# A head norm's sums issued behind the next product, row maxima spaced one by one, and their transposes some products later

## The chip, the cores and the metric

The kernel runs on one core of one Trainium2 chip. The metric is the device time of one execution in microseconds; of several runs the median is given, with the lowest and the highest.

## The reference

One inference step of a small hybrid model, on a prompt of 1024 tokens and a sample of 32 new tokens that has 1024 cached ones. Layer 0 mixes tokens with a state-space scan, layer 1 with multi-head latent attention; a gated per-layer embedding follows each. The change concerns the prompt's attention in layer 1 alone. Cut to what matters (16 heads, 64 plain and 32 rotated columns of a query or key, chunks of 64 tokens):

```python
q = (rmsnorm(q_a, q_a_norm) @ q_b_w).reshape(b, T, MLA_HEADS, MLA_QK)
q_nope = rmsnorm(q[..., :MLA_NOPE], qn_norm)
q_rope = apply_rope(rmsnorm(q[..., MLA_NOPE:], qr_norm), cos[:, None], sin[:, None])
kv = (lat_all @ kv_b_w).reshape(b, Tk, MLA_HEADS, MLA_NOPE + MLA_V)
k_nope = rmsnorm(kv[..., :MLA_NOPE], kn_norm)
...
s = (jnp.einsum('bqhd,bkhd->bhqk', qn, k_nope)
     + jnp.einsum('bqhd,bkd->bhqk', qr, k_rope)).astype(F32) * scale
mask = k_chunk[None, :] <= (qp // CHUNK)[:, None]
p = jax.nn.softmax(jnp.where(mask, s, -jnp.inf), axis=-1).astype(v.dtype)
return jnp.einsum('bhqk,bkhd->bqhd', p, v)
```

So each head's query and key are normed per token over the head's columns (the head norm), and each query's scores need the maximum of its row before the exponential.

## The kernel before, in words

**Numbers.** Nearly all products are of fp32 operands split into a high part that TensorE takes in one pass and a low rest (names with h and l, types fp32r): high by high, high by low and low by high are summed. A matmul on plain fp32, such as the norm's sum, shows as two records in the trace.

**Stages.** Layer 0, its output and its embedding fill the span up to 1078 us; then comes the attention's input projection, then `phase_sample` (the sample's attention), then `phase_prompt`, the prompt's, and after it the output projection and the last embedding.

**The order of work.** The kernel's text emits instructions; a scheduler then fixes the order on each engine. It plans along a simulated time and takes, of what is ready, what was emitted first. So the order of emission sets priorities, not the order itself. Buffers are given out by tag: tiles of one tag share `bufs` places, and a tile waits until a place is free. In the prompt's attention PSUM has four tags of two banks each: "mm" (products of preparation, the sums of head norms, values), "st" (scores), "s1" (row-max products and the transposes of maxima) and "o" (outputs).

**Preparation.** `Prompt.prep(p)` makes queries and keys of head pair p: two weights, two halves of 512 tokens each, so four products. For each, `gemm` (L245) fills a bank, `head_sq` (L900, L901) has ScalarE copy it to `hx` and square it to `hsq`, and `head_norm` (L910 to L913) sums the squares over each head by a matmul with a block-diagonal matrix into another bank of "mm", takes the reciprocal root on ScalarE (a logarithm and an exponential, L182 and L183) and multiplies on VectorE. `Prompt.rope_block(g)` does the same for the rotated columns of four heads (two products), then swaps halves by eight DMAs on SyncE and rotates. Both are generators that yield after each product. The first pair's preparation runs inside `phase_sample`, with products in the tag "st" there.

**Operands.** Two sets of buffers `qk` alternate between pairs. `fill(p)` puts the prepared halves into them: ScalarE writes the high parts (L1263), a DMA on GpSimd's queue the rotated rows (L1264), VectorE or GpSimd the low parts (L1268).

**Row maxima.** `row_max(i, par)` treats one head: for each of 8 blocks of 128 queries, one or two products of high parts (L1307), each followed by a maximum on VectorE (L1309): twelve in all, four blocks with one, four with two. It yields after each block, eight times. At its end a small reduction (L1311), a transpose on TensorE (L1313), a copy with the sign turned on ScalarE (L1315) and a DMA on GpSimd's queue (L1316) put the row of maxima into the low query operand `ql`, as a row of its own, so that the score product subtracts it.

**A head.** `head` walks twelve pieces: three score products (L1327), the exponential on ScalarE (L1333), the high part `ph` on ScalarE or VectorE (L1345, L1347), the rest `pl` on GpSimd or VectorE (L1348), three products with the values (L1350 to L1352; one fp32 product at L1341 for two of the eight key blocks). It yields after each piece.

**Interleaving.** For each pair p, `spread` merges three streams by position: the 24 pieces of pair p, the row maxima of pair p+1 (16 steps), and the preparation of pair p+2 (4 steps, 6 with a rope block). Step k of n stands at (k + 0.5)/n, less a lead of 0.05 for the last two. What a stream has left then runs in `run`, at the end. After odd pairs `values` (L1279) makes the values of the next four heads.

Of the kernel before, what the change touches and what calls it, by code (L numbers as in the profile page):

```python
# [10 lines left out]
F32 = mybir.dt.float32  # L11
# [6 lines left out]
P = 128  # L18
# [136 lines left out]
class Pools:  # L155


    def __init__(self, rest, **tags):
        self.rest, self.tags = rest, tags
# [32 lines left out]
def load_weight(c, src, nk, m, scale=None, eng_h=None, wp=None, wr=None):  # L192
    nc = c.nc
    wp = wp or c.wp
    raw = (wr or wp).tile([P, nk, m], F32, tag="wraw", name="wraw")
    nc.sync.dma_start(raw, src)
    if scale is not None:
        nc.gpsimd.tensor_tensor(raw, raw, bc_last(scale, m), op=ALU.mult)
    wh = wp.tile([P, nk, m], F32R, tag="wh", name="wh", bufs=c.whb)
    wl = wp.tile([P, nk, m], F32R, tag="wl", name="wl", bufs=c.whb)  # L200
    if eng_h:
        eng_h.tensor_copy(wh, raw)
    else:
        nc.scalar.activation(wh, raw, AF.Copy)  # L204
    nc.gpsimd.tensor_tensor(wl, raw, wh.bitcast(F32), op=ALU.subtract)  # L205
    return wh, wl
# [55 lines left out]
def pvc(c, name, i=0, n=1, rows=P):  # L262
    o, _ = PV[name]
    return c.pv[:rows, o + i : o + i + n]
# [631 lines left out]
def head_sq(c, ps, x, pool=None):  # L896

    n = x.shape[-1]
    sq = (pool or c.pre).tile([P, 352 if pool else 512], F32, tag="hsq", name="hsq", bufs=2)[:, :n]
    c.nc.scalar.activation(x, ps, AF.Copy)  # L900
    c.nc.scalar.activation(sq, ps, AF.Square)  # L901
    return sq


def head_norm(c, x, sq, w, bd):

    nc = c.nc
    n = x.shape[-1]
    pn = c.ps.tile([P, 512], F32, tag="mm", name="hn", bufs=2)
    nc.tensor.matmul(pn[:, :n], bd[0], sq, start=True, stop=True)  # L910
    r = c.pre.tile([P, 512], F32, tag="hr_", name="hr_", bufs=2)
    rsqrt(nc, c, r[:, :n], pn[:, :n], 1.0 / bd[1], c.eps)
    nc.vector.scalar_tensor_tensor(x, x, w, r[:, :n], op0=ALU.mult, op1=ALU.mult)  # L913
# [248 lines left out]
class Prompt:  # L1162


    def __init__(self, c, st):
        self.c, self.st, self.x = c, st, {}
        self.tag = "st"

    def rope_block(self, g):
        c, nc, I = self.c, self.c.nc, self.c.I  # L1170
        w = load_weight(c, I["qrW"][g], 3, P)
        rope = c.pre.tile([P, 2, 1024], F32, tag="rope", name="rope")
        sw, fq = rope[:, 0], rope[:, 1]
        for a in range(2):
            cols = slice(512 * a, 512 * a + 512)
            ps = c.ps.tile([P, 512], F32, tag=self.tag, name="psr", bufs=2)
            gemm(c, ps, w, self.st.qan, cols)
            head_norm(c, fq[:, cols], head_sq(c, ps, fq[:, cols]), pvc(c, "qr"), (c.bd32, 32))
            yield
        for h in range(4):  # L1180
            lo, hi = slice(32 * h, 32 * h + 16), slice(32 * h + 16, 32 * h + 32)
# [12 lines left out]
        nc.scalar.activation(h, fq, AF.Copy)  # L1194
        nc.vector.tensor_tensor(l, fq, sw, op=ALU.subtract)
        self.rope = rope.bitcast(F32R)

    def prep(self, p):

        c, I = self.c, self.c.I  # L1200
        self.x[p] = out = []
        for wsrc, nk, acts, wn in ((I["qnW"][p], 3, self.st.qan, "qn"), (I["kW"][p], 2, self.st.latp, "kn")):
            w = load_weight(c, wsrc, nk, P)
            for a in range(2):
                ps = c.ps.tile([P, 512], F32, tag=self.tag, name="psqk", bufs=2)
                gemm(c, ps, w, acts, slice(512 * a, 512 * a + 512))
                x = c.pre.tile([P, 512], F32, tag="hx", name="hx", bufs=6)
                head_norm(c, x, head_sq(c, ps, x), pvc(c, wn), (c.bd64, 64))
                out.append(x)
                yield  # L1210


def run(*gens):
    for g in gens:
        for _ in g:
            pass


LEAD = 0.05


def spread(*streams):

    order = sorted(((k + 0.5) / n - lead, i) for i, (_, n, lead) in enumerate(streams) for k in range(n))
    for _, i in order:
        next(streams[i][0], None)
    run(*(g for g, _, _ in streams))


def phase_prompt(c, st, pr, before):  # L1230
    nc, tc, I, O = c.nc, c.tc, c.I, c.O
    es = ExitStack()
    ap_ = es.enter_context(tc.tile_pool(name="att", bufs=1, reuse_waits="tile"))
# [4 lines left out]
    bufs = []  # L1238
# [55 lines left out]
            out.append((vh, vl))  # L1294
        return out

    def row_max(i, par):
        qk = bufs[i]
        qh, ql, kh, kl = (qk[n][par] for n in ("qh", "ql", "kh", "kl"))
        mrow = gap_rows(par, i).start + 10  # L1300
        mx = ap_.tile([P, 16], F32, tag="mx", name="mx", bufs=2)
        for b in range(8):
            n = max(256, 128 * (b + 1))
            ng, w = (1, n) if n <= 512 else (2, n // 2)
            for a in range(ng):
                ps = c.ps.tile([P, 512], F32, tag="s1", name="s1", bufs=2)
                nc.tensor.matmul(ps[:, :w], qh[:, 128 * b : 128 * b + 128], kh[:, a * w : a * w + w], start=True, stop=True)  # L1307
                col = b if b < 4 else 2 * b + a
                nc.vector.tensor_reduce(mx[:, col : col + 1], ps[:, : (w if b else 128)], axis=AX.X, op=ALU.max)  # L1309
            yield  # L1310
        nc.vector.tensor_reduce(mx[:, 4:8], mx[:, 8:16].rearrange("p (a b) -> p a b", b=2), axis=AX.X, op=ALU.max)  # L1311
        pm = c.ps.tile([P, 512], F32, tag="s1", name="pm", bufs=2)
        nc.tensor.transpose(pm[:8, :128], mx[:, 0:8], c.ident)  # L1313
        mr = ap_.tile([8, 128], F32R, tag="mr", name="mr", bufs=2)
        nc.scalar.activation(mr, pm[:8, :128], AF.Copy, scale=-1.0)  # L1315
        nc.gpsimd.dma_start(ql[mrow : mrow + 1, :], mr)  # L1316

    def head(vt, i, par, opair):
        qk = bufs[i]
# [42 lines left out]
    def pair(p, vt, opair):  # L1362
        for par in range(2):
            yield from head(vt, p % 2, par, opair)

    operands(0)
    fill(0)
    run(row_max(0, 0))
    operands(1)
    vt = values(0)  # L1370
    run(row_max(0, 1))
    run(pr.prep(1))
    for p in range(8):
        g, i = p // 2, p % 2
        opair = ap_.tile([P, 1024], F32, tag="op", name="op")
        sg = aq.tile([P, 1024], F32, tag="sg", name="sg")
        nc.sync.dma_start(sg, c.sg_d[p][:, :1024])
        streams = [(pair(p, vt, opair), 24, 0.0)]
        if p < 7:
            fill(p + 1)  # L1380
            streams.append((itertools.chain(row_max(1 - i, 0), row_max(1 - i, 1)), 16, LEAD))
        if p < 6:
            streams.append((itertools.chain(pr.prep(p + 2), pr.rope_block(g + 1) if i == 0 else ()), 6 if i == 0 else 4, LEAD))
        spread(*streams)
        if i == 1 and p < 7:
# [8 lines left out]
def build(tc, nc, I, O, dbg=None, ngroups=8, upto=9):  # L1394
# [4 lines left out]
    with ctx:  # L1399
# [175 lines left out]
```

## Time and profile before

| what | us |
|---|---|
| median of 3 runs | 1998.89 |
| lowest, highest | 1995.81, 2002.09 |
| the profiled execution, its own time | 1996.68 |
| its span | 1994.9 |
| TensorE busy (matmuls) | 1921.6 |
| VectorE, ScalarE, GpSimd busy | 1254.2, 1051.0, 955.6 |

The profile is of one execution. PE is TensorE's matmuls, PEld its weight loads, DVE is VectorE, ACT ScalarE, POOL GpSimd, SP SyncE. L1307 is line 1307 of the kernel before. A group's row gives the engine, the operation, output and inputs by their names, shapes and count, then busy time, mean ns of one, the idle time in front of it and what ended most of that. A row of waits gives who waited for whom, the total in us, the times, the longest. A row of the order in time gives start and duration in us. Matmuls are pipelined, so that a matmul's record still runs when the next one has started.

### The profile page before, as it was taken

To read this page: it belongs to the slowest core of one execution; us is meant where nothing else is said; L and a number is where in the kernel's file an instruction comes from. 1 tells how busy PE (TensorE), PEld (TensorE's weight loads), DVE (VectorE), ACT (ScalarE), POOL (GpSimd) and SP (SyncE) were. 2 spreads that over 40 slices of the span, in tenths; PEclk is the share of its full clock that TensorE was granted. 3 is DMA by queue.
4 is the path that set the end of the run, shared out by engine and by line. 5 is a ranking of instruction groups with operands and counts; after the bars stand their busy time and mean duration, and the time that the engine had idled before them with its cause. 6 is when DMAs were issued, how large, how long until landed. Compare 5 with 4: busy or idle time off the path is not lost. (4 is left out here: it accounts for less than half of the span.)

```text
span 1994.9 us, 32715 instructions
## 1 busy us (share of the span) xinstructions
PE 1921.6 (96%) x12811; PEld 1766.3 (89%) x12811; DVE 1254.2 (63%) x1613; ACT 1051.0 (53%) x1958; POOL 955.6 (48%) x811
## 2 busy tenths in 40 slices
PE   8999999999999999999998999998999999899999
PEld 6988899999999998989998999677778777779999
DVE  7888675746657575452377443364777887976544
ACT  5436555455545557342334341777687877754331
POOL 5642524343443545555777452124445454545772
PEclk9999999999999999999999999999999999999999
DMA  4134333424233347553233221434331311316442
GB/s 141 54 86 99 87 87 104 91 78 98 74 95 88 77 119 254 161 181 122 94 125 113 84 73 69 160 107 129 78 79 43 80 40 38 121 45 199 123 130 71
DMA packets 110730, 204.26 MB, mean 102 GB/s; under 512 B 18224, under 2 KB 60720, under 8 KB 110448
## 3 DMA queue, kind: packets, MB, share of 16 engines
q1 hardware_dynamic: 105472, 193.17, 33.0%
q0 software_dynamic: 2800, 6.91, 1.8%
q8 instruction: 100, 1.64, 0.3%
q10 hardware_dynamic: 2304, 2.10, 0.3%
q14 instruction: 54, 0.44, 0.1%
HBM read 156.81 MB, written 38.83 MB: 98 GB/s over the span
## 5 line engine op out<-in xcount | busy, mean ns | idle before, releaser
L205 POOL TENSOR_TENSOR wl<-wraw,wh 128x1024 fp32r<-128x1024 f32 (+3 forms) x183 | 373.4, 2042 | 424.0 <-ACT wh L204 386.2
L245 PE MATMUL mm<-hh,wl 128*128 128x384 f32 (+1 forms) x1136 | 372.7, 328 | 0.0
L245 PE MATMUL mm<-hh,wh 128*128 128x384 f32 (+1 forms) x1136 | 372.0, 328 | 0.0
L245 PE MATMUL mm<-hl,wh 128*128 128x384 f32 (+1 forms) x1136 | 370.8, 326 | 0.0
L245 PE MATMUL pso<-yhl,wh 128*128 128x264 f32 x1536 | 282.2, 285 | 4.7 <-DVE yhl L259 2.9
L204 ACT ACTIVATE wh<-wraw 128x1024 fp32r<-128x1024 f32 (+3 forms) x181 | 157.2, 869 | 245.8 <-PE pso L245 111.6
L245 PEld LDWEIGHTS pso<-yhl,wh 128*128 128x128 f32 x1536 | 238.5, 188 | 6.2 <-DVE yhl L259 4.0
L245 PE MATMUL pso<-yhl,wl 128*128 128x264 f32 x768 | 218.6, 285 | 3.9 <-POOL wl L205 3.9
L245 PEld LDWEIGHTS mm<-hh,wh 128*128 128x128 f32 x1136 | 214.6, 189 | 3.2 <-issue 2.8
L245 PEld LDWEIGHTS mm<-hl,wh 128*128 128x128 f32 x1136 | 214.8, 189 | 1.3 <-issue 0.5
L245 PEld LDWEIGHTS mm<-hh,wl 128*128 128x128 f32 x1136 | 214.6, 189 | 0.7 <-issue 0.2
L496 DVE SCALAR_TENSOR_TENSOR cx<-raw,pv,cx 128x1060 f32<-128x1060 f32 x96 | 142.6, 1490 | 42.6 <-ACT cx L494 42.0
L245 PE MATMUL psi<-yhl,wh 128*128 128x264 f32 x832 | 154.7, 287 | 4.1 <-ACT yhl L258 3.7
L559 ACT ACTIVATE ex<-ex,tokT 128x128 f32<-128x128 f32 (+1 forms) x288 | 87.0, 380 | 132.9 <-DMA ex<-acs_d 123.8
L245 PEld LDWEIGHTS pso<-yhl,wl 128*128 128x128 f32 x768 | 144.5, 188 | 4.6 <-POOL wl L205 4.6
L245 PE MATMUL pg<-hH,wl 128*128 128x264 f32 x512 | 145.9, 285 | 1.3 <-POOL wl L205 1.3
L245 PE MATMUL pg<-hH,wh 128*128 128x264 f32 x512 | 145.9, 285 | 0.0
L245 PE MATMUL pg<-hL,wh 128*128 128x264 f32 x512 | 145.6, 285 | 0.0
L1327 PE MATMUL st<-qk 128*128 128x512 f32 (+2 forms) x576 | 139.6, 358 | 1.5 <-DMA qk<-mr 0.9
L245 PEld LDWEIGHTS psi<-yhl,wh 128*128 128x128 f32 x832 | 130.7, 190 | 5.1 <-ACT yhl L258 3.9
L1348 POOL TENSOR_TENSOR pl<-pf,ph 128x512 fp32r<-128x512 f32 x64 | 81.8, 1278 | 104.7 <-DVE ph L1347 93.8
L572 POOL TENSOR_TENSOR hm<-hT,cd_all 128x256 f32<-128x256 f32 x64 | 53.1, 830 | 162.3 <-DVE hT L574 96.1
(539 smaller groups left out, 4666.5 us busy)
## 6 DMA issues: line engine op xcount, KB each, us to landing
wraw<-in_inW SPq DMA_DIRECT2D x48, 512.0 KB, 3.5
ex<-acs_d SPq DMA_DIRECT2D x32, 512.0 KB, 5.5
wraw<-in_outW SPq DMA_DIRECT2D x32, 512.0 KB, 3.7
yraw<-y_d SPq DMA_DIRECT2D x32, 264.0 KB, 4.6
u<-u_d SPq DMA_DIRECT2D x32, 264.0 KB, 2.8
eb<-ea_d SPq DMA_DIRECT2D x64, 128.0 KB, 4.0
y_d<-y SPq DMA_DIRECT2D x16, 512.0 KB, 2.8
wraw<-in_gateW SPq DMA_DIRECT2D x16, 512.0 KB, 3.6
```

The costliest lines, as they stand in the source:

```text
L204: nc.scalar.activation(wh, raw, AF.Copy)
L205: nc.gpsimd.tensor_tensor(wl, raw, wh.bitcast(F32), op=ALU.subtract)
L245: c.nc.tensor.matmul(ps, ww[:, k, :m], aa, start=first and k == 0 and i == 0, stop=last and k == n - 1 and i == 2)
L496: nc.vector.scalar_tensor_tensor(xh, raw[:, k : k + T1], pvc(c, "cw", 4 * b + k), xh, op0=ALU.mult, op1=ALU.add)
L559: nc.scalar.activation(e_, e_, AF.Relu, scale=-1.0, bias=tok(32)[:, i, h : h + 1])
L572: nc.gpsimd.tensor_tensor(hm.rearrange("p (h q) -> p h q", q=64), hT.rearrange("p (h q) -> p h q", q=64), bc_last(cd_all[:, hs, ch], 64), ...
L1327: nc.tensor.matmul(ps[:, :n], a_[:, ks], b_[:, q], start=t == 0, stop=t == 2)
L1348: (nc.gpsimd if idx in L_POOL else nc.vector).tensor_tensor(pl[:, :n], pf[:, :n], ph[:, :n].bitcast(F32), op=ALU.subtract)
```

## The change

The head norm of a product is kept back: `norm_later` first issues the norm that is waiting, and then keeps the new one; `norm_now` issues what is left at the end of `prep` and of the two products of `rope_block`. As its arguments are worked out first, the copy and the square of a product still come right behind it; the matmul that sums the squares, the reciprocal root and the multiplication come behind the next product and its square.

`row_max` yields after each product with its maximum, twelve times a head. The transpose, copy and DMA move into `max_row`. `row_maxima` runs both heads of a pair and calls `max_row` for the first after three products of the second, and for the second after two more empty steps.

`spread` gives each stream a stretch of its own: the pieces 0 to 1, the row maxima 26 steps from -0.03 to 0.9, the preparation from -0.05 to 0.95. At the start the first twelve row maxima are issued before the operands and values, and the rest, with both transposes, behind them.

```diff
             gemm(c, ps, w, self.st.qan, cols)
-            head_norm(c, fq[:, cols], head_sq(c, ps, fq[:, cols]), pvc(c, "qr"), (c.bd32, 32))
+            self.norm_later(fq[:, cols], head_sq(c, ps, fq[:, cols]), pvc(c, "qr"), (c.bd32, 32))
             yield
+        self.norm_now()
...
-                head_norm(c, x, head_sq(c, ps, x), pvc(c, wn), (c.bd64, 64))
+                self.norm_later(x, head_sq(c, ps, x), pvc(c, wn), (c.bd64, 64))
                 out.append(x)
                 yield
+        self.norm_now()
+
+    def norm_later(self, *a):
+
+        self.norm_now()
+        self.norms.append(a)
+
+    def norm_now(self):
+        if self.norms:
+            head_norm(self.c, *self.norms.pop())
...
 def spread(*streams):
 
-    order = sorted(((k + 0.5) / n - lead, i) for i, (_, n, lead) in enumerate(streams) for k in range(n))
+    order = sorted((a + (b - a) * (k + 0.5) / n, i) for i, (_, n, a, b) in enumerate(streams) for k in range(n))
...
                 nc.vector.tensor_reduce(mx[:, col : col + 1], ps[:, : (w if b else 128)], axis=AX.X, op=ALU.max)
-            yield
+                yield
         nc.vector.tensor_reduce(mx[:, 4:8], mx[:, 8:16].rearrange("p (a b) -> p a b", b=2), axis=AX.X, op=ALU.max)
+
+    def max_row(i, par, mx):
+
+        mrow = gap_rows(par, i).start + 10
         pm = c.ps.tile([P, 512], F32, tag="s1", name="pm", bufs=2)
         nc.tensor.transpose(pm[:8, :128], mx[:, 0:8], c.ident)
         mr = ap_.tile([8, 128], F32R, tag="mr", name="mr", bufs=2)
         nc.scalar.activation(mr, pm[:8, :128], AF.Copy, scale=-1.0)
-        nc.gpsimd.dma_start(ql[mrow : mrow + 1, :], mr)
+        nc.gpsimd.dma_start(bufs[i]["ql"][par][mrow : mrow + 1, :], mr)
+
+    def row_maxima(i):
+
+        mx = [ap_.tile([P, 16], F32, tag="mx", name="mx", bufs=2) for _ in range(2)]
+        yield from row_max(i, 0, mx[0])
+        for k, _ in enumerate(row_max(i, 1, mx[1])):
+            if k == 2:
+                max_row(i, 0, mx[0])
+            yield
+        yield
+        yield
+        max_row(i, 1, mx[1])
...
     operands(0)
     fill(0)
-    run(row_max(0, 0))
+    ahead = row_maxima(0)
+    for _ in range(12):
+        next(ahead)
     operands(1)
     vt = values(0)
-    run(row_max(0, 1))
+    run(ahead)
     run(pr.prep(1))
...
-        streams = [(pair(p, vt, opair), 24, 0.0)]
+        streams = [(pair(p, vt, opair), 24, 0.0, 1.0)]
         if p < 7:
             fill(p + 1)
-            streams.append((itertools.chain(row_max(1 - i, 0), row_max(1 - i, 1)), 16, LEAD))
+            streams.append((row_maxima(1 - i), 26, -0.03, 0.9))
         if p < 6:
-            streams.append((itertools.chain(pr.prep(p + 2), pr.rope_block(g + 1) if i == 0 else ()), 6 if i == 0 else 4, LEAD))
+            streams.append((itertools.chain(pr.prep(p + 2), pr.rope_block(g + 1) if i == 0 else ()), 6 if i == 0 else 4, -0.05, 0.95))
```

More of the change, by code (lines that the diff above doesn't have):

```diff
@@ L1167, in __init__ @@
         self.tag = "st"
+        self.norms = []
     def rope_block(self, g):
@@ L1216, in run @@
             pass
-LEAD = 0.05
 def spread(*streams):
-    order = sorted(((k + 0.5) / n - lead, i) for i, (_, n, lead) in enumerate(streams) for k in range(n))
+    order = sorted((a + (b - a) * (k + 0.5) / n, i) for i, (_, n, a, b) in enumerate(streams) for k in range(n))
     for _, i in order:
         next(streams[i][0], None)
-    run(*(g for g, _, _ in streams))
+    run(*(x[0] for x in streams))
 def phase_prompt(c, st, pr, before):
@@ L1295, in values, with row_max @@
         return out
[L1297 to L1301, printed above, removed]
+    def row_max(i, par, mx):
+        qh, kh = (bufs[i][n][par] for n in ("qh", "kh"))
         for b in range(8):
```

## The prediction, made before the changed kernel was run

> **What bounds the kernel.** I read the page first: the span and the busy shares.
>
> ```profile
> span 1994.9 us, 32715 instructions
> PE 1921.6 (96%) x12811; PEld 1766.3 (89%) x12811; DVE 1254.2 (63%) x1613; ACT 1051.0 (53%) x1958; POOL 955.6 (48%) x811
> ```
>
> TensorE is busy for 96% of the span, and the change adds and removes no product. So it can only gain what TensorE waits where the change works, and lose by new waits. I then cut the span by where row-max and score products appear: the sample's attention runs up to 1394 us, a start without full pairs up to 1436, the eight pairs of heads up to 1800. The view by stretches shows these, pair 6, and a short stretch inside it.
>
> ```profile
> core 0: us, PE busy (x) PEld busy (x) DVE busy (x) ACT busy (x) POOL busy (x), PEclk, DMA share, GB/s
> 1250.00:1394.00 144.00, 132.89 (x693) 103.98 (x691) 71.71 (x135) 110.97 (x270) 39.96 (x61) 0.99 0.46 133
> 1436.00:1800.00 364.00, 347.29 (x1700) 274.92 (x1699) 290.61 (x487) 266.07 (x533) 182.69 (x189) 0.99 0.23 61
> 1724.00:1766.00 42.00, 36.32 (x173) 28.01 (x172) 39.30 (x61) 26.07 (x53) 24.77 (x23) 0.92 0.38 122
> 1737.00:1750.00 13.00, 9.51 (x32) 6.37 (x33) 12.42 (x16) 4.55 (x10) 9.49 (x6) 0.74 0.26 84
> ```
>
> The pairs take 364 us with TensorE busy in 347.29: 16.7 us idle is the order of everything that can be won there. VectorE is busy for 290.61, or 80%. In pair 6 it is 39.30 of 42, so there VectorE sets the pace. The view of waits from 1394 to 1805 tells who ended TensorE's idle time; first the matmuls' own, then the weight loads', which see a wait earlier because a matmul's tail hides the start of it.
>
> ```profile
> PE s L1307 <- DVE mx L1309: 5.4, 8, 1.6
> PE o L1351 <- POOL pl L1348: 3.0, 5, 2.1
> PE o L1350 <- DVE ph L1347: 2.5, 2, 1.8
> PE o L1351 <- DVE pl L1348: 2.5, 3, 1.5
> PE hn L910 <- ACT hsq L901: 2.2, 3, 1.0
> ...
> PEld s L1307 <- DVE mx L1309: 10.3, 18, 2.0
> PEld hn L910 <- ACT hsq L901: 3.5, 4, 1.4
> ```
>
> The change aims at two rows: row-max products that wait for VectorE's maximum (5.4 to 10.3 us) and the norm's sum that waits for ScalarE's square (2.2 to 3.5 us). The others, 8.0 us, belong to the softmax pieces, which it doesn't touch. The order on each engine is not that of the text: a scheduler fills it in from simulated times, with the order of emission as priority. The change moves emission, so it moves all of this plan.
>
> **Part 1, the norm behind the next product.** In the prompt both use the tag "mm", with two banks. In the trace a norm's sum and the next product run back to back, after the square of the product before:
>
> ```profile
> 1565.98 0.59 ACT L901 ACTIVATE hsq<-psqk 128x512 f32<-128x512 f32 x1
> 1568.53 1.02 PE L910 MATMUL hn<-hsq,bd 128*128 128x512 f32 x2
> 1568.99 0.79 PE L245 MATMUL psqk<-qanH,wh 128*128 128x512 f32 x1
> ...
> 1585.04 0.59 ACT L901 ACTIVATE hsq<-psqk 128x512 f32<-128x512 f32 x1
> 1585.69 1.13 PE L910 MATMUL hn<-hsq,bd 128*128 128x512 f32 x2 [0.95 <-ACT hsq L901]
> ```
>
> The square ends at 1566.57, the sum starts at 1568.53 and the next product at 1568.99. I read it so: product N holds one bank until its square has read it, sum N takes the other, and product N+1 needs the first. After the change the order of allocation is product N+1, sum N, product N+2, so in the steady run product N+2 still waits for square N+1: the wait of 2.2 to 3.5 us passes from the sum to a product. Gain between 0 and 3.5 us; I take 0. Only where a pair has few other products ready (as at 1585.69) would it be more. In the sample's attention the prompt's first six products use the tag "st", and there the sum really leaves their path:
>
> ```profile
> PE hn L910 <- ACT hsq L901: 3.1, 6, 1.2
> PEld hn L910 <- ACT hsq L901: 4.9, 6, 1.4
> ```
>
> Of the 30 sums in that stage 24 are the sample's own, which already come one product later, and 6 are the prompt's: a fifth of 3.1 us is 0.6. Gain between 0 and 4.9, I take 0.5. The six instructions of a norm (two matmul records, logarithm, exponential, product) stay what they are. What moves farthest is the last norm of a stream: it now comes only when the pair's other streams have been emitted, and behind it the rope's eight swaps on SyncE, its VectorE products, and the next operands' DMAs on GpSimd. Its price is in the rival on lateness.
>
> **Part 2, maxima one at a time.** Of a head's twelve products, eight came two to a step. Now each of 24 has its own step, over a stretch from -0.03 to 0.9 of the pair with two empty steps behind: the last at -0.03 + 0.93 x 23.5/26 = 0.81 of the pair instead of 15.5/16 - 0.05 = 0.92.
>
> ```profile
> L1309 DVE TENSOR_REDUCE mx<-s 128x1 f32<-128x128 f32 (+2 forms) x192 | 102.4, 550 | 26.7 <-PE s L1307 25.8
> ```
>
> A maximum takes 0.55 us and there are two banks, so two products at once leave the third waiting up to 1.1 us for VectorE, more when a cast stands ahead. At one per step this shrinks by about half, not to nothing, because VectorE stays 80% busy. Gain between 0 and 10.3; I take half of the upper row, 5.2. What is late next is the cast ph on VectorE (2.5 us above), which the same reductions delay.
>
> **Part 3, the transposes later.** Sixteen transposes, ScalarE copies and DMAs on GpSimd stay. For the first head they come at step 15 of 26 (0.49) instead of step 9 of 16 (0.48), but behind three more products; for the second, at the end of emission as before. The wait that this may spare is on GpSimd:
>
> ```profile
> L1316 POOL DMA_DIRECT2D qk<-mr x16 | 9.3, 582 | 9.1 <-ACT mr L1315 7.2 <-ACT pf L1333 1.7
> ```
>
> GpSimd sits 7.2 us in front of this DMA, and behind it in its queue stand the pl subtractions for which TensorE waits 3.0 us. Gain between 0 and 3.0, I take 0.5.
>
> **Part 4, pair 6.** There the two reductions of a step stand ahead of a cast, and TensorE runs dry:
>
> ```profile
> 1736.31 0.68 DVE L1348 TENSOR_TENSOR pl<-pf,ph 128x512 fp32r<-128x512 f32 x1
> 1738.62 1.27 DVE L1309 TENSOR_REDUCE mx<-s 128x1 f32<-128x512 f32 x2
> 1739.82 1.38 DVE L1347 CAST ph<-pf 128x512 fp32r<-128x512 f32 x1
> 1741.31 2.66 DVE L1348 TENSOR_TENSOR pl<-pf,ph 128x512 fp32r<-128x512 f32 x1
> ...
> 1741.26 0.49 PE L1350 MATMUL o<-ph,vh 128*128 128x512 f32 x1 [1.81 <-DVE ph L1347]
> 1744.02 0.80 PE L1351 MATMUL o<-pl,vh 128*128 128x512 f32 x1 [1.46 <-DVE pl L1348]
> ...
> 1740.88 2.54 POOL L205 TENSOR_TENSOR wl<-wraw,wh 128x1024 fp32r<-128x1024 f32 x1
> ```
>
> One reduction out of the way is 1.27/2 = 0.6 us: I take that, of 3.3 us (1.81 + 1.46) at most. The same pl took 0.68 us and, while a GpSimd subtraction of 2.54 us ran, 2.66. The Trainium skill (SBUF — State Buffer, "Who interferes with whom") says that a VectorE instruction with two SBUF inputs contends with a GpSimd one that reads SBUF, and that the one issued second is blocked. The trace agrees: pl was issued 0.43 us after the subtraction and ended 0.55 us after it. By that rule spacing the maxima spares nothing of the second wait, and Part 4 would stay at 0.6 at best.
>
> **The sum.** 0 + 0.5 + 5.2 + 0.5 + 0.6 = 6.8 us gained, and 0.5 us given back for last norms that come late (bounds 0 and 12, below): 6.3 net. The profiled execution took 1996.68 us, its span and 1.8 around it, and so would take 1990.4. The median of the three runs, 1998.89, is 2.2 above it, so I predict 1992.6 us. About 0.3%, 6.0 us, is what a measurement of this kernel can tell from no change.
>
> **Rivals.** *The waits only move* (chance 0.33). A sum's wait passes to a product, and the maxima wait at a VectorE that is 80% busy whatever their spacing; for it speaks that two banks remain for each. Then only 0 to 5 us come: 1994 to 1999, centre 1996.5.
>
> *The maxima arrive late* (chance 0.22), the slower side. A head's scores need its row of maxima, and before an even pair it is there just in time:
>
> ```profile
> 1619.40 0.27 PE L1313 MATMUL pm<-cst,mx 128*8 128x128 f32 x1
> 1620.71 0.40 PE L1327 MATMUL st<-qk 128*128 128x512 f32 x1
> 1621.41 0.28 PE L1279 MATMUL psv<-wh,lpH 128*128 128x256 f32 x1
> 1624.24 0.55 POOL L1316 DMA_DIRECT2D qk<-mr  x1
> ...
> DMA to landing us min/median/max: 1.6/1.7/6.8
> ```
>
> At 1620.71 pair 4's first score product is out, but the row's DMA is only issued at 1624.24 and lands 1.7 us later. Until then TensorE works on values (psv) and the next pair's products. Three row-max products more ahead of the transpose are some 4 us there (they follow the DMA of rotated rows, which the last norm delays too). If the cover falls short, pairs 2, 4 and 6 each pay up to 4 us: 12 us, or 2010.9 at most; with Part 2's 5.2 us still gained it is 6.8 us, 2005.7. It decides once the delay is longer than the values and products left, about 5 us after the first score. Against it: after pairs 1 and 3 ten products of the next pair follow the values. That is why I charge only 0.5.
>
> *The jam in pair 6 dissolves* (chance 0.10). From 1737 to 1750 the granted clock was 0.74, so 0.26 x 13 = 3.4 us of array time were lost behind those two waits. If a new plan keeps TensorE fed there, that comes back with the 3.3 us of waits, less the 0.6 counted: 6.1 us, 1986.5. The Trainium skill (TensorE: Matmul & The Clock Gate, "Why this matters for your kernels") advises no idle gap over about 3 us, since an idle window halves the clock. Here gaps of 1.81 and 1.46 us close together sufficed.
>
> **Numbers.** The forecast, 5 to 10 us gained by spaced maxima, has 0.35. Faster by over 0.3%: 0.35 + 0.10 = 0.45. Within 0.3%: 0.33. Slower by over 0.3%: 0.22. The range takes in the dissolved jam with the rest of Part 1's bound in the sample on one side (1986.5 less 4.4, 1982) and the late maxima on the other (2006). The forecast's own range is 1989 to 1994.
>
> **What would show it.** Right: in the waits of this stage the row for s behind mx falls to about half, hn behind hsq goes and a like wait appears at psqk behind hsq; the idle time of 16.7 us in the pairs falls to about 10. Wrong: the mx row stays, or st waits for the DMA of mr at pairs 2, 4 and 6, or waits for ph and pl grow by more than the mx row loses.

## The result and the profile after

The changed kernel takes 2009.2 us (median of six runs, 2007.8 to 2012.9) against 1998.4 for the kernel before (six runs, 1995.8 to 2002.1): ratio 1.0055, 95% interval 1.0044 to 1.0067. It is 10.8 us slower, where 6.3 us faster was forecast, and above the 2006 us at which the prediction's range ends. The profiled execution took 2007.83 us. The head of its page, then the view by stretches of after and of before, with edges where each kernel's row maxima and scores begin and end (and pair 6 of after as the third row):

```profile
span 2006.0 us, 32748 instructions
```

```profile
1394.00:1424.00 30.00, 17.79 (x70) 14.91 (x71) 12.51 (x21) 7.11 (x13) 7.24 (x11) 0.67 0.79 176
1424.00:1808.00 384.00, 369.16 (x1792) 291.12 (x1792) 304.72 (x523) 281.36 (x568) 186.25 (x199) 0.98 0.22 60
1733.00:1780.00 47.00, 41.30 (x203) 32.88 (x203) 40.15 (x68) 28.05 (x57) 25.46 (x26) 0.89 0.36 113
```

```profile
1394.00:1403.00 9.00, 8.38 (x46) 7.09 (x47) 5.96 (x9) 2.42 (x7) 3.82 (x6) 1.00 0.40 112
1403.00:1796.00 393.00, 374.55 (x1821) 294.71 (x1819) 312.33 (x527) 287.64 (x577) 198.07 (x207) 0.99 0.24 65
```

The span is 11.1 us longer, but the loss is not spread. From the first score product to the last, the eight pairs take 384 us after and 393 before: there the time is shorter. In front of them stands a new stretch of 30 us in which TensorE is busy for 17.79 us at a mean clock of 0.67; before, 9 us lay between the sample's attention and the first score product, at full clock. The views of single tiles give the marks exactly: the prompt's first product (psqk), the first row-max product (s), the first and the last score product (st), first before, then after.

```profile
L245 PE MATMUL psqk<-qanH,wh x48: 389/397/798, 1258.4 to 1665.4; 128*128 128x512 f32 x48
L1307 PE MATMUL s<-qk x192: 277/364/794, 1394.6 to 1775.6; 128*128 128x384 f32 x48, 128*128 128x512 f32 x48, 128*128 128x256 f32 x32, 128*128 128x320 f32 x32
L1327 PE MATMUL st<-qk x576: 274/389/1202, 1402.9 to 1795.7; 128*128 128x512 f32 x102, 128*128 128x256 f32 x64, 128*128 128x384 f32 x26
```

```profile
L245 PE MATMUL psqk<-qanH,wh x48: 389/397/793, 1258.8 to 1679.5; 128*128 128x512 f32 x48
L1314 PE MATMUL s<-qk x192: 275/365/792, 1422.8 to 1784.6; 128*128 128x384 f32 x48, 128*128 128x512 f32 x48, 128*128 128x256 f32 x32, 128*128 128x320 f32 x32
L1350 PE MATMUL st<-qk x576: 274/389/798, 1423.3 to 1808.4; 128*128 128x512 f32 x98, 128*128 128x256 f32 x64, 128*128 128x384 f32 x30
```

Up to psqk after is 0.4 us later. From there to the first score product it takes 164.5 us instead of 144.5: 20.0 us lost. From the first score product to the last, 385.1 instead of 392.8: 7.7 us gained. Behind it, to the end of the span, 197.6 instead of 199.2: 1.6 gained. 0.4 + 20.0 - 7.7 - 1.6 = 11.1.

Part of the loss and of the gain is the same work on the other side of the mark, for the change removes no product: 30 of the first 48 products of values (psv) stand ahead of the first score product in after and none before, and four row-max products moved the other way. The views by stretches between these marks tell it apart. Ahead of the first score product TensorE is busy 7.9 us more (134.22 before, 142.15 after) and idle 12.1 us more (10.28, 22.35). From the first score product to the last it is busy 4.1 us less (374.35, 370.26) and idle 3.6 us less (18.45, 14.84).

The waits of the new stretch (engine, line, tile, releaser: us in total, times, longest) say what ends last:

```profile
PE psv L1288 <- DVE vl L1302: 5.0, 1, 5.0
PE s L1314 <- DMA qk<-rope: 3.1, 1, 3.1
PE psv L1288 <- ACT wh L204: 2.5, 1, 2.5
```

The first row-max product waits for the DMA that puts the rotated rows of the first rope block into the pair's buffers; until it lands TensorE has only values (psv) and the sample's last group, and these wait for VectorE and ScalarE. The view of the tile rope follows that block, before and then after:

```profile
L1182 SPq DMA_DIRECT2D rope<-rope x4: 512/548/950, 1305.3 to 1314.7; - x4
L1264 POOL DMA_DIRECT2D qk<-rope x2: 557/562/567, 1385.6 to 1386.2; - x2
L913 DVE SCALAR_TENSOR_TENSOR rope<-rope,pv,hr__13355 x1: 733/733/733, 1304.6 to 1304.6; 128x512 f32<-128x512 f32 x1
L1195 DVE TENSOR_TENSOR rope<-rope x1: 1215/1215/1215, 1326.4 to 1326.4; 128x1024 fp32r<-128x1024 f32 x1
```

```profile
L1184 SPq DMA_DIRECT2D rope<-rope x4: 518/587/587, 1395.5 to 1399.3; - x4
L1273 POOL DMA_DIRECT2D qk<-rope x4: 527/536/537, 1415.4 to 1417.0; - x4
L913 DVE SCALAR_TENSOR_TENSOR rope<-rope,pv,hr__14316 x1: 743/743/743, 1394.8 to 1394.8; 128x512 f32<-128x512 f32 x1
L1197 DVE TENSOR_TENSOR rope<-rope x1: 1224/1224/1224, 1413.9 to 1413.9; 128x1024 fp32r<-128x1024 f32 x1
```

The block's last multiplication (L913) moved from 1304.6 to 1394.8, and with it the swaps on SyncE (1305 to 1395), the split (1326 to 1414) and the DMA into qk (1385.6 to 1415.4). Before, the split was done 58 us ahead of that DMA, and the chain lay hidden beside the sample's attention. After, it runs in the open. Its head in the timeline: the sum on TensorE before, then after, then ScalarE after.

```profile
1299.95 1.13 PE L910 MATMUL hn<-hsq,bd 128*128 128x512 f32 x2 [0.66 <-ACT hsq L901]
```

```profile
1384.03 1.10 PE L1113 MATMUL pz<-ut,wv 128*128 128x64 f32 x8 [1.10 <-ACT ut L1108]
1384.97 1.08 PE L910 MATMUL hn<-hsq,bd 128*128 128x512 f32 x2
```

```profile
1388.61 2.13 ACT L1258 ACTIVATE qk<-krt 32x1024 fp32r<-32x1024 f32 x2
1390.65 0.66 ACT L182 ACTIVATE hr__14316<-hn,eps 128x512 f32<-128x512 f32 x1
1392.34 0.61 ACT L183 ACTIVATE hr__14316<-hr__14316 128x512 f32<-128x512 f32 x1
```

In after the sum runs directly behind the third group's last product of the sample (pz), which stands ahead of it in the order of emission and uses banks of the same tag, mm. Its logarithm then stands on ScalarE behind the copies of the operands, 4.6 us after the sum's end. In the pairs the rows that the prediction watched look so in after, from 1424 to 1814, the matmuls' own and then the weight loads':

```profile
PE s L1314 <- DVE mx L1316: 4.8, 4, 2.3
PE hn L910 <- ACT hsq L901: 0.3, 1, 0.3
PE psqk L245 <- ACT hsq L901: 0.2, 1, 0.2
...
PEld s L1314 <- DVE mx L1316: 9.0, 15, 2.6
PEld psqk L245 <- ACT hsq L901: 1.5, 3, 0.7
```

hn behind hsq is nearly gone, and a like wait of 0.2 to 1.5 us stands at psqk. The mx row has hardly moved: 4.8 and 9.0 for 5.4 and 10.3. Of the 3.6 us that TensorE is idle less there, the matmuls' own row of hn gives 1.9, for which the forecast took 0, and that of mx 0.6, for which it took 5.2.

### The profile page after: what moved, and what is told of

It reads as the page before. It is cut to its first block, busy times and chain, and to the rows that moved or that the text cites. A ratio compares the mean times of both kernels' runs of the same rounds, so it can differ in the third digit from the quotient of the medians.

```text
span 2006.0 us, 32748 instructions
## 1 busy us (share of the span) xinstructions
PE 1926.9 (96%) x12811; PEld 1773.0 (88%) x12811; DVE 1249.2 (62%) x1613; ACT 1049.0 (52%) x1958; POOL 946.0 (47%) x811
## 5 line engine op out<-in xcount | busy, mean ns | idle before, releaser
L1350 PE MATMUL st<-qk 128*128 128x512 f32 (+2 forms) x576 | 143.9, 364 | 1.0 <-ACT pf L1356 0.8
L1371 POOL TENSOR_TENSOR pl<-pf,ph 128x512 fp32r<-128x512 f32 x64 | 75.8, 1184 | 127.9 <-DVE ph L1370 122.9
L1316 DVE TENSOR_REDUCE mx<-s 128x1 f32<-128x128 f32 (+2 forms) x192 | 104.1, 550 | 48.3 <-PE s L1314 46.7
```

The source lines that it names most:

```text
L1350: nc.tensor.matmul(ps[:, :n], a_[:, ks], b_[:, q], start=t == 0, stop=t == 2)
L1371: (nc.gpsimd if idx in L_POOL else nc.vector).tensor_tensor(pl[:, :n], pf[:, :n], ph[:, :n].bitcast(F32), op=ALU.subtract)
```

## The experiments

First theory: the late last sum of the first rope block holds the first pair's rotated rows back, and that is the loss. Rivals: the new start (twelve row-max products, then values, then the others), rows of maxima that come late in the pairs, or the deferral itself, wherever it is done. Second question: which edit gains in the pairs. Every ratio is to runs of the kernel before on the same chip; their medians were 1999.6 (first group of runs), 2000.1, 2000.7 and 1999.2.

### The parts alone

x1_first_rope is after with one edit in `rope_block`:

```diff
+            if g == 0 and a == 1:
+                self.norm_now()
             yield
```

> The kernel after, with one norm put back: the second sum of the first rope block (the one in the sample's attention) is issued at once. Theory 'late first rope': in the kernel after this sum ran at 1385.0 us instead of 1301.9, the first row-max product at 1422.8 instead of 1394.6, and from the second pair on the kernel after is 8.8 us shorter (307.1 against 315.9). So this kernel gets the start back and keeps the pairs: about 1998.4 - 9 = 1989 us, the first row-max product near 1395. Theory 'split start' (the 28 us come from twelve row maxima ahead of the values and twelve behind them): 2009, first row-max product still near 1423. Theory 'late maxima' (my rival on record: rows of maxima land late before the pairs 2, 4 and 6): 2009 as well, since the pairs are as in the kernel after.

Measured: 1999.0 us, ratio 1.0002 (0.9983 to 1.0021). One sum issued at its old place brings 10 us back; the first row-max product is at 1402.7 instead of 1422.8. Some 8 us remain to x4, below.

x3_norm_only is the kernel before with `norm_later` and `norm_now` and nothing else of the change.

> The kernel before with the norm's delay alone; row maxima, transposes and the merge of streams as before. 'Late first rope': the start is lost as in the kernel after (first row-max product near 1420, some 20 us), and the pairs gain 0 to 3 us, because a product still needs the bank that the square before it frees: 2015 to 2019 us. If the norm's delay also shortens the pairs, as the 8.8 us may come from it: about 2009. 'Split start' and 'late maxima': 1998, since neither is in this kernel.

Measured: 2020.8 us, ratio 1.0109 (1.0089 to 1.0130), above both expectations. The deferral alone costs 21 us.

x4_maxima_only is after with both `self.norm_later(...)` put back to `head_norm(c, ...)`: the maxima and their transposes as changed, no deferral.

> The kernel before with everything but the norm's delay: spaced row maxima, later transposes, the new stretches of the merge, the split start. 'Late first rope': no loss at the start (first row-max product near 1395) and the pairs' 8.8 us kept if they come from the maxima: about 1989 us; if they come from the norm: 1998. 'Split start': the start is lost, 2009 or more. 'Late maxima': slower than before, 2001 to 2010, by waits of score products for the DMA of the row.

Measured: 1991.3 us, ratio 0.9960 (0.9949 to 0.9971). The other half of the change gains 8.3 us and beats both kernels. Its first row-max product stands at 1396.7. The rival "new start" falls here: x4 has that start too.

x5_norm_only_first_rope is x3 with x1's edit.

> The kernel before with the norms deferred everywhere but for the first rope block's second sum, which is issued at once; maxima as before. If the late rotated rows are the whole price of the deferral: 1999 us, as the kernel before (the deferral alone took 2020.8). If a part of the price comes from the deferral in the pairs, as the difference between 1999.0 with the rope's sum at once and 1991.3 with no deferral suggests: 2004 to 2012.

Measured: 2002.7 us, ratio 1.0020 (1.0005 to 1.0034), between the two expectations and 18 us under x3 with that one sum back in place.

x12_one_late_sum turns this round: x4 with one single norm late (the lines are against x4).

```diff
-            head_norm(c, fq[:, cols], head_sq(c, ps, fq[:, cols]), pvc(c, "qr"), (c.bd32, 32))
+            if g == 0 and a == 1:
+                self.norm_later(fq[:, cols], head_sq(c, ps, fq[:, cols]), pvc(c, "qr"), (c.bd32, 32))
+            else:
+                head_norm(c, fq[:, cols], head_sq(c, ps, fq[:, cols]), pvc(c, "qr"), (c.bd32, 32))
             yield
         self.norm_now()
```

> The kernel that took 1991.3 us with one single norm moved: the second sum of the first rope block comes after the sample's last group, every other norm at once. If that one sum is the loss at the start: first row-max product at 1420 to 1430 and 2010 to 2019 us (19 to 27 us above, as start and whole took with all six deferred). If it needs the other five deferred with it: 1991 to 2000.

Measured: 2017.4 us, ratio 1.0081 (1.0061 to 1.0102). The views of the tiles rope and s in x12:

```profile
L913 DVE SCALAR_TENSOR_TENSOR rope<-rope,pv,hr__14316 x1: 742/742/742, 1400.2 to 1400.2; 128x512 f32<-128x512 f32 x1
L1317 PE MATMUL s<-qk x192: 276/364/794, 1427.1 to 1793.4; 128*128 128x384 f32 x48, 128*128 128x512 f32 x48, 128*128 128x256 f32 x32, 128*128 128x320 f32 x32
```

One of the prompt's 40 norms (four for each of eight pairs, two for each of four rope blocks), moved alone, costs 26 us against x4 by the medians and 24 by the ratios. Its multiplication and the first row-max product come even 5.4 and 4.3 us later than in after, and from the first prompt product to the first score product x12 takes 165.9 us, x4 144.1. This settles the first question.

### Place in the order, or the bank

x9_step_more keeps the whole deferral and moves only where the stream's rest is emitted:

```diff
         next(ahead, None)
         next(up, None)
+    run(ahead)
     nc.sync.dma_start(latt[:, 0:8], I["latt"])
```

> The kernel after with the whole deferral kept, and the rest of the stream that runs ahead (the last sum of the first rope block and its rotation) emitted right behind its sixth step instead of after the sample's last group. If what costs is where that sum stands in the order of emission: first row-max product back from 1423 to 1396-1403 us, 1991 to 2000 us. If the deferral itself costs, wherever its last sum stands: 2005 to 2010.

Measured: 2003.5 us, ratio 1.0011 (0.9997 to 1.0025); between the two expectations. In the trace the start is back, as the first theory says:

```profile
L913 DVE SCALAR_TENSOR_TENSOR rope<-rope,pv,hr__13371 x1: 751/751/751, 1305.9 to 1305.9; 128x512 f32<-128x512 f32 x1
L1315 PE MATMUL s<-qk x192: 276/364/798, 1401.4 to 1778.8; 128*128 128x384 f32 x48, 128*128 128x512 f32 x48, 128*128 128x256 f32 x32, 128*128 128x320 f32 x32
```

From the first prompt product to the first score product it takes 148.1 us (144.5 before, 164.5 after). What x9 still loses to x4 lies ahead of the first score product (x4 takes 144.1 there) and in the pairs: 393.0 us from first to last score product, x4 386.2.

x6_bank_s1 is after with that one sum in a bank of tag s1 (`head_norm(..., tag="s1")` in place of `norm_now` for the first block).

> The kernel after, with the late sum of the first rope block left as late in emission as it is, but in a bank of the tag s1 (the sample's key products) instead of mm (its transposes, outputs and sums). In the kernel after the sum ran 0.4 us behind the last product of the sample's third output group, the last user of mm ahead of it in emission. If the order of banks holds it back ('bank'): it runs right behind the last key product, near 1367 us, and the first row-max product comes 15 to 18 us earlier than 1422.8; the time is 1995 to 2003. If its late place in emission alone makes it wait for idle time on TensorE ('priority'): it stays near 1385 and the time at 2009.

Measured: 2003.9 us, ratio 1.0024 (1.0005 to 1.0043), just above what a queue for banks alone was expected to give. The timeline of TensorE in x6 around its sums, and the view of the tile rope:

```profile
1369.13 1.02 PE L910 MATMUL hn<-hsq,bd 128*128 128x512 f32 x2
```

```profile
L913 DVE SCALAR_TENSOR_TENSOR rope<-rope,pv,hr__14316 x1: 751/751/751, 1376.4 to 1376.4; 128x512 f32<-128x512 f32 x1
```

With another tag the sum runs at 1369.1 instead of 1385.0, but not near 1300, where it stood before. So the queue for mm's banks made 16 of the 85 us. The rest goes with the place of emission behind the sample's groups, as x9 shows; how much of it is a queue for s1's banks, which the sample's key products use, x6 can't tell. The first row-max product comes at 1409.7, 13 us earlier than in after, and the time falls by 5 us only: 1376 is still too late to hide the chain.

### The deferral in the sample and in the pairs

x7_sample_defer and x8_pairs_defer split the deferral by stage, with one edit each in `norm_later`: behind `self.norms.append(a)`, x7 calls `norm_now` at once if the tag is "mm", x8 if it is "st".

> The kernel after with the deferral only where the prompt's products use the banks of tag st, that is in the sample's attention (six products, the late sum of the first rope block among them); in the pairs each norm follows its product at once. If the late rotated rows are the whole price: 2009, as after. If the deferral in the pairs costs something of its own: 2001 to 2005. First row-max product near 1423 us in both.

Measured: 2018.3 us, ratio 1.0087 (1.0054 to 1.0121): above both expectations.

> The kernel after with the deferral only in the pairs (tag mm); in the sample's attention each norm follows its product at once. If the late rotated rows are the whole price: 1991, as with no deferral. If the deferral in the pairs costs something of its own: 1996 to 2000, as with only the rope's sum at once (1999.0). First row-max product near 1396 in both.

Measured: 1996.5 us, ratio 0.9991 (0.9976 to 1.0005). The deferral in the pairs costs 5.2 us where the start is on time (x8 over x4), and gains 9.1 where it is late (after under x7), by the medians. From the first prompt product to the end of the span the profiled runs differ by 4.8 and 5.3 us; x7's stands 5.5 us behind after's already at that product, up to which the kernels do the same. I expected one sign; it is no property of the edit alone, but depends on the plan that it meets. In x8 the waits of s behind mx are 8.7 us, where x4 has 1.7, half of it in one place. Rows of the timeline of x8 there:

```profile
1744.37 3.70 DVE L259 TENSOR_TENSOR yhl<-yraw,yhl 128x528 fp32r<-128x528 f32 x1
1745.14 2.36 POOL L205 TENSOR_TENSOR wl<-wraw,wh 128x1024 fp32r<-128x1024 f32 x1
1749.25 2.24 DVE L1318 TENSOR_REDUCE mx<-s 128x1 f32<-128x512 f32 x4
1749.99 1.68 PE L1316 MATMUL s<-qk 128*128 128x320 f32 x3 [4.07 <-DVE mx L1318]
```

The maxima stand behind a VectorE subtraction that takes 3.70 us while GpSimd subtracts too; the median of its group of 48 is 0.71. That looks like the jam of pair 6, met at another point.

x13_prep_only is x8 with `head_norm` at once in the rope blocks.

> The deferral only in the pairs and only for the operands' norms; the sums of the rope blocks 1 to 3 at once too (deferral in all of the pairs took 1996.5, no deferral 1991.3). If the 5 us between these come from late rotated rows in the pairs: 1991 to 1993. If they come from the order of the operands' products: 1995 to 1999.

Measured: 1993.1 us, ratio 0.9964 (0.9950 to 0.9977). Of x8's 5.2 us, 3.3 go with the three rope blocks and 1.8 stay with the operands, though single runs of these kernels lie 3 us and more from their medians, and the intervals of x13 and x4 overlap. That is a share, not a mechanism.

### What gains in the pairs

x10_rows_at_once and x11_two_a_step take x4 apart. x10 keeps one product to a step and the new stretch, with each transpose right behind its twelfth product (24 steps for 26; the lines are against x4, and the `yield` left out behind the twelfth product is not shown):

```diff
-        yield from row_max(i, 0, mx[0])
-        for k, _ in enumerate(row_max(i, 1, mx[1])):
-            if k == 2:
-                max_row(i, 0, mx[0])
+        for par in range(2):
+            yield from row_max(i, par, mx[par])
+            max_row(i, par, mx[par])
             yield
-        yield
-        yield
-        max_row(i, 1, mx[1])
```

> No deferral (as the kernel that took 1991.3 us), maxima one at a time over the new stretch, but each head's transpose and row right behind its twelfth product. By the prediction's split (5.2 us for the spacing, 0.5 us for later transposes): 1991 to 1993. If the later transposes carry the gain: 1997 to 2000, as before.

Measured: 1998.3 us, ratio 0.9990 (0.9977 to 1.0003). The two traces say why: listed by tile and form, buffer numbers left out, the 12811 matmuls of x10 stand in the same order as before, and from the first prompt product to the end of the span the two kernels take 736.4 and 736.5 us. Spacing the emission over the new stretch changed the order of no matmul, as far as these names tell.

x11 moves the `yield` of `row_max` back out of its inner loop and has the transpose behind two products (18 steps over the new stretch):

> No deferral, transposes some products later and the new stretch, but the products two to a step as in the kernel before. If the spacing of the maxima carries the gain: 1996 to 2000, and the wait of row-max products for maxima back from 1.7 to about 5 us. If the later transposes or the earlier stretch do: 1990 to 1993.

Measured: 1991.9 us, ratio 0.9962 (0.9947 to 0.9977). So the prediction's split is upside down: spacing without later transposes gains nothing that can be told, later transposes without spacing, over the new stretch, gain 8.7 us. The waits of s behind mx, matmuls and weight loads, in x10 and in x11:

```profile
PE s L1314 <- DVE mx L1316: 5.6, 7, 1.6
PEld s L1314 <- DVE mx L1316: 10.2, 18, 2.0
```

```profile
PE s L1314 <- DVE mx L1316: 2.1, 4, 0.7
PEld s L1314 <- DVE mx L1316: 6.4, 14, 1.0
```

x14_rows_later_only is the kernel before with x11's two `max_row` calls and nothing else: two products to a step, `LEAD` and 16 places in the merge as before. At the start, too, the first head's transpose comes later.

> The kernel before with the transposes alone moved: the first head's behind two products of the second, the second's behind two empty steps; products two to a step, stretch and lead as before, no deferral. If the later transposes carry the whole gain, because the next head's row-max products no longer queue behind a transpose in the banks of tag s1: 1991 to 1994, and the pause of the row-max products between two heads of a pair falls from 4.7 us to about 2. If the earlier stretch is needed with it: 1996 to 2001.

Measured: 1994.7 us, ratio 0.9973 (0.9961 to 0.9985). Moved alone, the transposes gain 4.5 us by the medians and 5.4 by the ratio. The matmuls of x14 stand in the same order as those of x11, and from the first prompt product to the end of the span the two take 731.9 and 732.2 us, 4.6 and 4.3 less than before. So the new stretch does nothing in x11 either, and its 8.7 us and the 4.5 here are two measurements of one order on TensorE. The timeline's row-max products (s) and transposes (pm) around the middle of one pair, before (with the end of the chain of maxima on VectorE) and in x14:

```profile
1567.15 0.40 PE L1307 MATMUL s<-qk 128*128 128x512 f32 x1
1569.59 0.15 DVE L1311 TENSOR_REDUCE mx<-mx 128x4 f32<-128x8 f32 x1
1573.39 0.27 PE L1313 MATMUL pm<-cst,mx 128*8 128x128 f32 x1
1573.42 0.36 PE L1307 MATMUL s<-qk 128*128 128x256 f32 x1
```

```profile
1564.39 0.62 PE L1305 MATMUL s<-qk 128*128 128x512 f32 x2
1569.71 0.28 PE L1305 MATMUL s<-qk 128*128 128x256 f32 x1
1570.74 0.28 PE L1305 MATMUL s<-qk 128*128 128x256 f32 x1
1572.26 0.27 PE L1315 MATMUL pm<-cst,mx 128*8 128x128 f32 x1
```

Before, the second head's first product starts 6.27 us after the first head's last, right behind the transpose: both take banks of tag s1, and the transpose was emitted first. The maxima were ready at 1569.74, so the transpose stood 3.65 us longer where the scheduler had put it, and TensorE was busy with other products through the whole pause. In x14 two products go ahead of it. Over the seven pairs prepared so, this pause is 4.7 us on average before and in x10, 2.8 in x11 and x14, 1.8 in x4, 1.7 in x1 and x9, 1.5 in after (start of the first product of the second head less that of the last of the first, from the starts of the tile s).

x15_rows_later_still is x4 with `k == 6` for `k == 2`.

> The kernel that took 1991.3 us (no deferral) with the first head's transpose behind seven products of the second head in place of three. If three are cover enough for the chain of maxima: 1990 to 1993. If more cover still helps: 1986 to 1989. If rows then come too late for the scores: 1994 to 2003, with waits of st for the rows' DMA above the 2.7 us that they were with three.

Measured: 2000.0 us, ratio 1.0006 (0.9995 to 1.0016). The gain is gone, but not by late rows: the wait of st for the rows' DMA is 0.6 us, and that of s behind mx is 5.1 again, with a pause of 2.2 us. So a short pause is not enough (x1 and x9 have one, and their pairs take 392.7 and 393.0 us, before 392.8), and none of my theories forecast this. The profiled run, the fastest of the ten, takes 733.1 us from the first prompt product on, 3.4 less than before; no trace shows where the others lose that.

x16_rows_other_bank is x10 with `tag="mm"` for the bank of pm.

> Transposes right behind the twelfth product (the kernel that took 1998.3 us), but into a bank of tag mm, so that the next head's products don't queue behind them for the banks of tag s1. If that queue is what the later transposes spare: 1990 to 1994, and the pause between two heads about 2 us. If it is the place in the order of emission alone: 1996 to 2000, pause near 4.7 us as with tag s1.

Measured: 2031.2 us, ratio 1.0155 (1.0140 to 1.0171). The pause falls to 1.3 us, as a queue for s1's banks would have it, but the time rises by 32 us, outside both expectations: the operands' products, their sums and the values use mm too and would now queue behind the transposes, and the pause between the second head and the next pair's first grows from 6.5 us to 19.4. That the pause between the heads is a queue for s1's banks is shown; what it costs can't be read from this kernel alone.

## Why the prediction was wrong

**The step that failed** is in Part 1: "In the sample's attention the prompt's first six products use the tag "st", and there the sum really leaves their path", "Gain between 0 and 4.9, I take 0.5". It priced the sum's wait and not the place to which the last sum moves. The prediction did say that "the last norm of a stream" comes "only when the pair's other streams have been emitted" and that the rope's swaps, products and DMAs hang behind it, but it looked for the price at the pair boundaries ("0.5 us given back for last norms that come late (bounds 0 and 12, below)"). The stream ahead of the sample's attention has the same shape, and its rest is emitted by `run(ahead)` after the sample's third group. There the sum moved from 1300 to 1385, the cover of 58 us was gone, and 20.0 us were lost before the first score product, 12.1 of them as idle time of TensorE. x12 shows it alone (26 us over x4), x1 and x5 undo it (10 and 18 us back). The bound of 12 came from the pairs' rows and did not hold this.

**Part 1 in the pairs**, "I take 0": the wait did pass from the sum to the product (hn to 0.3 us, psqk at 0.2 to 1.5), as argued. The time moved by -9 to +5 us by the medians all the same, with the plan that the deferral met.

**Part 2**, 5.2 us for spaced maxima: in x10 the wait for mx stays at 5.6 and 10.2 us, since the order on TensorE stays as it was, and in after, too, "the mx row stays", the prediction's first sign of being wrong; the time of x10 falls by a quantity that can't be told from none. **Part 3**, 0.5 us for later transposes: x14 gives 4.5 (medians) to 5.4 (ratio), and x11, the same order, 8.7. The mx wait that Part 2 meant to halve falls by later transposes alone, to 2.1 and 6.4 us in x11. I had looked for Part 3's wait on GpSimd's queue and overlooked the order on TensorE, in which the second head's products queue for the banks of tag s1 behind the transpose. That pause was to be seen before: no row-max product between 1567.15 and 1573.42. It is not shown that the pause is what costs, as x15, x1 and x9 have it short and do not gain. The sum of the two terms, 5.7, came near what x4 gains (8.3), by luck: two errors against each other.

**Part 4**, 0.6 us in pair 6: it lasts from 1733.6 to 1779.8 in after, 46 us for 42 before. The last row of after's stretches above has the same 5.7 us of idle TensorE as before (47.00 less 41.30; 42.00 less 36.32), at a clock of 0.89 instead of 0.92. The jam moved and did not dissolve.

**The rivals.** The slower one, late maxima, gave nearly the time that came (2005.7 to 2010.9) by a mechanism that did not act: in after no wait of st for the rows' DMA is among those of the pairs, and in x4 it is 2.7 us. That the measured time lies in a rival's span is no evidence for it. What failed was the term of 0.5 for last norms that come late.

**What stays open:** why the deferral in the pairs gains behind a late start and costs behind an early one; by what way the later transposes gain, as the pause alone does not explain it; why seven products ahead of the transpose (x15) lose what three gain; and the 3 us that x1 and x9 still lose ahead of the first score product, while x5, with the same five sums deferred in the sample, loses none there.

## What to carry to other kernels

When a step is deferred to "behind the next one", look first at the last step of every stream: what is emitted in front of it, whose banks it queues for, and how long its chain of users (here swaps, products, split, DMA) was hidden; one norm of 40 decided this change. Where two kinds of work take buffers of one tag, the one emitted first holds the other back, so try a few products of the other ahead of one that waits for a long chain; then measure how many, for here two or three gained and seven did not. When an edit of the emission changes nothing, compare the order on the engine first: in x10 it was the old order. When a change has two parts, price and run each alone: this one was a gain of 8 us and a loss of 21 in one diff, and the first without the second (x4, 1991.3 us) has the lowest median of all these kernels, though x11 (1991.9) and x13 (1993.1) can't be told from it.

## What the runs showed of the hardware

A TensorE that worked in two bursts around a wait got its clock back only behind the second. The view by stretches of after, around the late start, and two rows of its timeline:

```profile
1405.00:1420.00 15.00, 7.41 (x30) 6.62 (x30) 8.37 (x11) 5.77 (x10) 6.52 (x10) 0.54 0.90 225
```

```profile
1415.61 0.58 PE L1288 MATMUL psv<-wh,lpH 128*128 128x256 f32 x1 [4.97 <-DVE vl L1302]
1419.42 0.29 PE L1288 MATMUL psv<-wl,lpH 128*128 128x256 f32 x1
```

From 1405 to 1420 the mean granted clock is 0.54 although TensorE is busy half of the time: from 1407.2 to 1410.6 and, behind a wait of 4.97 us, from 1415.6 to 1419.7. Products of values take some 0.41 us each in both bursts (the first of each 0.58), where their median before was 0.28; the first to be as short again is the one at 1419.42, 3.8 us after the second burst began. At a mean clock of 0.67 over the stretch of 30 us, 0.33 x 30 = 9.9 us of array time are lost there, part of them in the 12.2 us that TensorE is idle anyway. The Trainium skill (TensorE: Matmul & The Clock Gate, "What's actually happening") says that full rate comes back after about 3.4 us of sustained work; the trace agrees, with 3.4 us ahead of the wait that were not enough and 3.8 us behind it that were.

In before's pair 6 a shorter wait was enough to lose the clock. It was full (1.00) from 1738.4 to 1741.8, with TensorE busy for 1.59 of these 3.40 us, and half (0.50) from 1742 to 1745. It fell behind the wait of 1.81 us and ahead of that of 1.46, which ended at 1744.02; so of the prediction's "gaps of 1.81 and 1.46 us close together" only the first can have had a part in that.

In after the DMA engines were busy for 0.90 of the time from 1405 to 1420. The rotated rows' DMA, issued at 1415.4, was waited for until 1422.8, 7.4 us. Before, it was 9.0 us from that DMA's issue at 1385.6 to the first row-max product at 1394.6, so in after it was late and not slow.
